# A refitted planner, a layernorm in steps and an in-place split in a two-layer hybrid backbone kernel

## The chip, the cores and the metric

The kernel is one program on one core of a Trainium2 chip. It has five engines with an instruction queue each: PE (TensorE, matrix products; its weight loads are shown as PEld), DVE (VectorE), ACT (ScalarE), POOL (GpSimd) and SP (SyncE, which issues most DMAs). The metric is the device time of one execution in microseconds (us), the median of several runs.

## The reference

Two layers act on 256 latent tokens and 256 context tokens of width 1024. Each layer modulates both streams, forms one wide input projection, runs four bidirectional mixers, merges their outputs by gates and adds a ConvFFN, each half closed by a residual layernorm:

```python
for i in range(DEPTH):                                   # DEPTH = 2
    zl = _split_cols(_modulate(x, sh1, sc1) @ w_in[i])
    zc = _split_cols(_modulate(h_ctx, csh1, csc1) @ w_in[i])
    ret_c, ret_l = _retention(zc, zl, n_rows)
    hg_c, hg_l = _hgrn2(zc, zl, ...)
    gd_c, gd_l = _gdn(zc, zl, ...)                       # gated delta rule: triangular solves
    lr_c, lr_l = _rglru(zc, zl, ...)
    y_l = _merge([ret_l, hg_l, gd_l, lr_l], zl['merge_gate'], w_branch[i], w_out[i])
    x = _layernorm(alpha * x + g1 * y_l, ln_mix_g[i], ln_mix_b[i])
    f_l = _conv_ffn(_modulate(x, sh2, sc2), w_up[i], ...)
    x = _layernorm(alpha * x + g2 * f_l, ln_ffn_g[i], ln_ffn_b[i])
    # the context stream likewise, in all layers but the last

def _merge(branches, gate_logits, w_branch, w_out):
    merged = sum(gates[:, :, j] * (branches[j] @ w_branch[j]) for j in range(4))
    return merged @ w_out
```

All of it is float32.

## The kernel before

**Products.** A float32 product is made of three products of a shorter type (float32r): both operands are split into a high part, rounded by ACT, and a low part, the difference. For the weights this goes tile by tile. SP loads a tile `wraw` (128 x 1024, 4 at a time), ACT rounds it to `wH`, and DVE or POOL subtracts: `wL = wraw - wH`. The thread `splitter` (line 332) does this some tiles ahead; 395 tiles need a split, and a split is 128 x 1024 elements except in the last products of an FFN (768) and the small `gd_ab` tiles (128). The engine is chosen by `tt` (line 671): DVE if the estimate of its end there, plus a bias, is below that on POOL. The names of the products on PE are `gft` and `gtf` (input projection, output projection and second FFN product), `up` (first FFN product) and `mg_b` (branch times `w_branch`).

**Order.** The program is one straight list, written by a planner at build time. Work is cut into threads (Python generators that yield the engine and the operands of the next step). `account` (line 150) keeps an estimated clock per engine, for every instruction as it is written; `pump` (line 244) picks the step that could start first by these clocks, and steps of matrix products where no thread's step can start before PE is free. So durations written into `account` decide where each instruction stands in each engine's queue, and through `tt`, on which engine it runs. On the chip each queue runs in that order, whatever the clocks were.

**Stages.** In time order: the start; layer 0's input products and mixers; its merge; `w_out` with the first residual layernorm; its FFN; the FFN's layernorm with the start of layer 1; the same stages of layer 1, the last of them a layernorm and the stores. In the mixers the gated delta rule inverts 32 x 32 triangular blocks by a chain of 60 POOL instructions each time (tiles `gd_x`, `gd_z`), four times in the program.

**Residual layernorm.** `gy = gtf * grow` and `r = r + gy` empty a bank of `w_out`'s (or the FFN's) products, `st` takes its statistics. When four are there, `ln_rs` computes the reciprocal deviation by some ten small DVE instructions (`rq`, `rq_v`, `rq_i`, `rq_n`), and `post_ln` (line 873) applies gain and bias to the two halves of `r`, four DVE instructions of 128 x 1024. In the old kernel `post_ln` is a plain function: these four are written at one go, and no other thread's step comes between them. Then `modulate` normalises again (`bst`, `xn`), transposes on PE (`xmt`) and splits (`xmH`, `xmL`).

**Merge.** For each of the four branches (order `lru`, `ret`, `gdn`, `hg`), `load` in `merge_jobs` (line 1007) fetches four blocks of it from DRAM into `br`, and splits each into `brH` (ACT) and `brL` (DVE or POOL). In the old kernel a block is loaded, then split, then the next comes; for the first two branches of layer 0 the DMAs stand in SP's queue, for the others in POOL's, between its splits. `prods` runs the products; DVE multiplies by the gates (`mg_th`) and adds to `merged`. Before it writes the next bank it finishes the bank before it, of the same branch.

Of the kernel before, what the change touches and what calls it, by code (L numbers as in the profile page):

```python
# [39 lines left out]
TRACE = 0  # L40
SUB_POOL = 1
POOL_BIAS = 0.3
# [5 lines left out]
SPLIT_BIAS = 0.3  # L48
ORDER = ("gdn0", "lru", "gdn1", "hg0", "hg1", "ret0", "ret1")
MERGE = ("lru", "ret", "gdn", "hg")  # L50
# by layer: the instances that follow one another in a pool
# [4 lines left out]
# the second layer's modulation blocks that fill the layernorms' waits  # L56
# [5 lines left out]
# from an engine's end to the start of the one that waits for it  # L62
# [9 lines left out]
class _Eng:  # L72
    """An engine of nc; every call also goes to the order's estimate of the engines' clocks."""
# [30 lines left out]
class _Pair:  # L104
    """the context's and the latents' jobs of one block"""
# [9 lines left out]
class Net:  # L115
    def __init__(self, nc, tc, I, out, n_tiles, dbg=None, stop=None):
# [9 lines left out]
        self.table, self.n_ran = "exp", 0  # L126
        self.jobs, self.fill, self.sel = [], [], []
# [5 lines left out]
    # ------------------------------------------- estimate of the engines' clocks  # L133
    def after(self, table, name, key):
        """when an engine sees that a tile is written (rdy) or read (rd)"""
        return max([t + LAT[p][key] for p, t in table.get(name, {}).items()] + [0.0])

    def names(self, x):
        """what the estimate knows an operand by: its tile, and the blocks of 256 for the activations"""
# [10 lines left out]
    def account(self, key, name, a, k):  # L150
# [12 lines left out]
        if not dma:  # L163
            # engines take turns at a PSUM tile
            for x in ins:
                if x.space == PSUM:
                    t = max([t] + [e for p, e in self.rd.get(x.tensor.name, {}).items() if p != key])
        by = key
        if key == "PE":
            if name == "transpose":  # L170
                d = 0.11
            elif ins[0].dtype == F32R:
                d = (n if n >= 256 else 4 * n) / 2400.0
            else:
                d = max(4 * n / 2400.0, 0.2)
                if out.ap[0][1] == 32:
                    d *= 0.28
        elif dma:
# [5 lines left out]
            d = out.ap[0][1] * n * 4 / 360e3  # L184
# [9 lines left out]
        elif key == "DVE":  # L194
# [5 lines left out]
            if name == "copy_predicated" and src_ps:  # L200
                e *= 0.85
            if name == "reciprocal":
                e *= 6
            if name == "tensor_reduce" or name.startswith("bn"):
# [4 lines left out]
            d = 0.07 + e + 0.06 * len(sc)  # L209
        else:  # L210
            d = 0.14 + n * 2.1e-3
        if not dma:
# [4 lines left out]
        for x in inn:  # L217
            q = self.rd.setdefault(x, {})
            q[by] = max(q.get(by, 0.0), t + d)

# [16 lines left out]
    # ------------------------------------------------------------- the order  # L237
# [33 lines left out]
    def finish(self, t, bank=False):  # L271
        """emit the rest of a thread, or its steps up to the last use of its bank"""
# [4 lines left out]
    def limit(self, key, n):  # L277
        """at most n threads of a kind are under way"""
# [5 lines left out]
    def when(self, t):  # L284
        """the engine of a thread's next step and the time when its operands are there (None: it waits for other steps)"""
# [8 lines left out]
    # -------------------------------------------------- matrix products' stream  # L294
# [20 lines left out]
    def feed(self):  # L315
        """keep loads three tiles ahead and splits two tiles ahead of the tile in use"""
# [15 lines left out]
    def splitter(self):  # L332
        """thread: the loaded tiles' two float32r parts, one tile ahead of the tile in use"""
# [15 lines left out]
    def gemm_start(self):  # L349
        """when the next step of the matrix products can start (None: it waits for a thread's step)"""  # L350
# [1872 lines left out]
```

## Time and profile before

| what | us |
|---|---|
| median of 3 runs | 2274.57 |
| lowest and highest run | 2270.27, 2276.27 |
| span of the profiled execution | 2267.0 |
| PE busy in it | 2085.0 |
| DVE busy | 1503.0 |
| ACT busy | 870.1 |
| POOL busy | 717.8 |

The span runs from the first to the last instruction, so the runs' times lie a few us above it; the profiled execution's own time is not given beyond its span. In all there are 35537 instructions. A busy share is a mean over stages: the rows below cut the span by stage, since the same engine may pace one stage and be idle in the next. "PEclk" or "clock" is the granted clock of PE as a share of 2.4 GHz; at its lower level, 1.2 GHz, it is 0.5.

### The profile page before, as it was taken

What the parts mean: (1) busy time and instruction counts of PE and PEld (TensorE: products, weight loads), DVE (VectorE), ACT (ScalarE), POOL (GpSimd) and SP (SyncE); (2) the same over time, 40 slices, a digit from 0 to 9 for tenths busy, and PEclk for the clock granted to TensorE, in tenths of its full rate; (3) what the DMA queues carried; (4) which work ended last, traced back from release to release, by engine and by line L of the source; (5) the groups of instructions that cost most, each with busy time, mean ns of one, the idle gap of its engine ahead of it and who ended that gap; (6) DMA issues with size and microseconds to landing.
All of it is one profiled execution on the core that took longest, in us unless ns stands there. A gap on an engine that the chain in (4) does not pass through costs nothing.

```text
span 2267.0 us, 35537 instructions
## 1 busy us (share of the span) xinstructions
PE 2085.0 (92%) x14052; PEld 1819.1 (80%) x14052; DVE 1503.0 (66%) x2380; ACT 870.1 (38%) x1277; POOL 717.8 (32%) x606
## 2 busy tenths in 40 slices
PE   6999899999999989879999986998998999888997
PEld 4767677877898968768898885887888889877997
DVE  6677346444383868976646688786375485878877
ACT  4555223222233233334423434664243323324553
POOL 1227422631130434420010032483247243513511
PEclk9999999999999999979999998999999999999999
DMA  7655325443314257554232344354234413566553
GB/s 296 202 171 161 126 64 161 120 148 103 120 64 136 83 174 248 160 176 128 91 98 93 98 154 159 111 161 139 83 120 129 135 33 98 177 234 209 180 187 118
DMA packets 133384, 320.14 MB, mean 141 GB/s; under 512 B 32961, under 2 KB 55265, under 8 KB 133217
## 3 DMA queue, kind: packets, MB, share of 16 engines
q1 hardware_dynamic: 119600, 289.76, 39.5%
q0 software_dynamic: 3712, 13.03, 1.8%
q10 hardware_dynamic: 9904, 15.08, 1.8%
q8 instruction: 111, 1.82, 0.3%
q14 instruction: 57, 0.46, 0.1%
HBM read 294.70 MB, written 23.10 MB: 140 GB/s over the span
## 4 chain that ended last, share of the span: by engine, by line
PE 64%; DVE 18%; POOL 5%; DMA 5%; issue 4%; ACT 3%; SPq 0%; ACTq 0%; DVEq 0%; POOLq 0%
PE gft L82 18%; PE gtf L82 15%; PE up L82 14%; PE mg_b L82 3%; DVE r L82 2%; POOL gd_x L82 2%; POOL gd_z L82 2%; DVE ffy L82 2%; DMA wraw<-in_wt 2%; PE hg_s L82 2%; DVE rq L82 2%; PE gd_U L82 2%; PE gd_o L82 2%; DMA br<-brd 1%; PE modp L82 1%
## 5 line engine op out<-in xcount | busy, mean ns | idle before, releaser
L82 POOL TENSOR_TENSOR wL<-wraw,wH 128x1024 fp32r<-128x1024 f32 (+2 forms) x143 | 335.7, 2351 | 890.3 <-ACT wH L82 756.5
L82 ACT ACTIVATE wH<-wraw 128x1024 fp32r<-128x1024 f32 (+2 forms) x395 | 408.0, 1036 | 216.2 <-PE gtf L82 130.5
L82 DVE TENSOR_TENSOR wL<-wraw,wH 128x1024 fp32r<-128x1024 f32 (+1 forms) x252 | 328.3, 1307 | 122.6 <-ACT wH L82 122.1
L82 PE MATMUL gft<-xmH,wH 128*128 128x512 f32 (+1 forms) x544 | 214.3, 398 | 3.8 <-ACT wH L82 3.8
L82 PE MATMUL gft<-xmL,wH 128*128 128x512 f32 (+1 forms) x544 | 205.5, 382 | 0.0
L82 PE MATMUL gft<-xms,wH 128*128 128x256 f32 x1344 | 188.3, 293 | 12.4 <-ACT lru_g L82 4.6
L82 PEld LDWEIGHTS gft<-xms,wH 128*128 128x128 f32 x1344 | 173.9, 198 | 18.1 <-ACT lru_g L82 4.8
L82 DVE SCALAR_TENSOR_TENSOR ffy<-up,parf,ffy 128x255 f32<-128x255 f32 (+1 forms) x188 | 110.9, 590 | 84.2 <-ACT ffy L82 79.5
L82 PE MATMUL up<-xmH,wH 128*128 128x512 f32 (+1 forms) x400 | 146.5, 373 | 13.6 <-DVE ffy L82 6.8
L82 PE MATMUL up<-xmL,wH 128*128 128x512 f32 (+1 forms) x400 | 146.1, 372 | 1.7 <-DVE xmL L82 1.7
L82 PEld LDWEIGHTS gft<-xmH,wH 128*128 128x128 f32 x544 | 103.7, 191 | 41.4 <-issue 16.7
L82 PE MATMUL gtf<-wH,hidH 128*128 128x256 f32 x528 | 132.0, 282 | 0.3 <-ACT wH L82 0.3
L82 PE MATMUL gtf<-wH,hidL 128*128 128x256 f32 x528 | 131.7, 282 | 0.0
L82 PE MATMUL gft<-xmH,wL 128*128 128x512 f32 (+1 forms) x544 | 131.3, 383 | 0.2 <-POOL wL L82 0.2
L82 PE MATMUL gtf<-wH,xmH 128*128 128x256 f32 x448 | 117.6, 294 | 9.6 <-DVE gy L82 9.0
L82 PEld LDWEIGHTS gft<-xmL,wH 128*128 128x128 f32 x544 | 103.8, 191 | 17.8 <-issue 0.7
L82 PEld LDWEIGHTS gft<-xmH,wL 128*128 128x128 f32 x544 | 98.2, 190 | 19.9 <-issue 1.3
L82 PE MATMUL gtf<-wH,xmL 128*128 128x256 f32 x448 | 113.6, 285 | 0.0
L82 ACT ACTIVATE ffy<-up,parf 128x256 f32<-128x256 f32 (+1 forms) x94 | 61.0, 648 | 120.2 <-PE up L82 120.0
L82 PE MATMUL mg_b<-brH,wH 128*128 128x256 f32 (+1 forms) x288 | 92.1, 338 | 13.4 <-ACT brH L82 9.1
L82 PEld LDWEIGHTS gtf<-wH,hidH 128*128 128x128 f32 x528 | 100.0, 189 | 0.6 <-ACT wH L82 0.5
L82 PEld LDWEIGHTS up<-xmH,wH 128*128 128x128 f32 x400 | 78.7, 197 | 26.7 <-issue 12.8
(335 smaller groups left out, 4677.9 us busy)
## 6 DMA issues: line engine op xcount, KB each, us to landing
wraw<-in_wt SPq DMA_DIRECT2D x467, 512.0 KB, 3.8
thd<-mg_t ACTq DMA_DIRECT2D x32, 256.0 KB, 2.2
mg_th<-thd SPq DMA_DIRECT2D x32, 256.0 KB, 4.1
wraw<-in_wt SPq DMA_DIRECT2D x20, 384.0 KB, 3.0
lnw<-in_rows POOLq DMA_DIRECT2D x8, 512.0 KB, 6.3
thd<-mg_t ACTq DMA_DIRECT2D x32, 128.0 KB, 2.6
xmm<-thd SPq DMA_DIRECT2D x16, 256.0 KB, 6.5
brd<-ro_b SPq DMA_DIRECT2D x28, 128.0 KB, 1.9
```

Of the source, the lines that this page charges most:

```text
L82: r = f(*a, **k)
```

## The change

1. `account` has other durations. A PE product takes 0.0135 us (float32r) or 0.01 us (float32) more, a change of PE's tiling mode 0.095 us, and `clocked` lets the estimated PE clock halve when it was idle. Two forms on DVE cost other amounts. `port` makes POOL instructions and DVE instructions with two SBUF operands (and single-operand `tensor_scalar` and copies) take turns in the estimate.
2. `POOL_BIAS` and `SPLIT_BIAS` go from 0.3 to -1.0: DVE is taken even if it would end up to 1 us later than POOL.
3. `post_ln` is a generator that yields before each half of `r`, so other steps can come between the halves; its callers use `yield from`.
4. A branch's block is loaded straight into the tile `brL`, all four DMAs first, and split in place; there is no `br` tile.
5. The bank before the next is finished across branches, too (`mlast`).

Docstrings and comments were also taken out, which the cut below leaves away.

```diff
-POOL_BIAS = 0.3
+POOL_BIAS = -1.0
-SPLIT_BIAS = 0.3
+SPLIT_BIAS = -1.0
...
         if key == "PE":
+            up = lambda z: 32 if z <= 32 else 64 if z <= 64 else 128
+            mode = up(ins[0].ap[0][1]), up(out.ap[0][1])
             if name == "transpose":
                 d = 0.11
             elif ins[0].dtype == F32R:
-                d = (n if n >= 256 else 4 * n) / 2400.0
+                mode = 128, 128
+                d = (n if n >= 256 else 4 * n) / 2400.0 + 0.0135
             else:
-                d = max(4 * n / 2400.0, 0.2)
+                d = max(4 * n / 2400.0, 0.2) + 0.01
                 if out.ap[0][1] == 32:
                     d *= 0.28
+            if mode != self.mode:
+                self.mode = mode
+                d += 0.095
+            d = self.clocked(t, d)
...
-            if name == "copy_predicated" and src_ps:
-                e *= 0.85
+            if name == "copy_predicated":
+                e = n * 1.13e-3
...
+            if name == "tensor_tensor_scan":
+                e = n * 2.1e-3
...
             d = 0.07 + e + 0.06 * len(sc)
+            if self.port_op(name, ins, sc):
+                t = self.port(key, t, d)
         else:
             d = 0.14 + n * 2.1e-3
+            t = self.port(key, t, d)
...
+    def clocked(self, t, d):
+        h, e = self.ham, t
...
+            f = 2.0 if h[2] else 1.0
...
+    def port(self, key, t, d):
+        q = self.turns
+        for k, s, e in q:
+            if k != key and s <= t < e:
+                t = e
+        q.append((key, t, t + d))
+        del q[:-6]
+        return t
...
         for j in range(2):
             x = r[:, j, :]
+            yield "DVE", [rs]
             V.scalar_tensor_tensor(x, in0=x, scalar=mv[:, j, 0:1], in1=self.lw[:, 0, :], op0=ALU.subtract, op1=ALU.mult)
...
-            st["L"] = self.tile(pool, [128, 4, n], F32R, "brL", "brL", nb)
+            st["L"] = self.tile(pool, [128, 4, n], F32, "brL", "brL", nb)
             for k in range(4):
-                b = self.ev([128, n], "br32") if early else self.tile(pool, [128, n], F32, "br32", "br32", 4)
-                (self.S if early else self.G).dma_start(b, self.brd[j][:, k, tsl])
-                yield "ACT", [b, st["H"]]
-                self.split(st["H"][:, k, :], st["L"][:, k, :], b)
+                (self.S if early else self.G).dma_start(st["L"][:, k, :], self.brd[j][:, k, tsl])
+            for k in range(4):
+                yield "ACT", [st["L"], st["H"]]
+                self.split(st["H"][:, k, :], st["L"][:, k, :].bitcast(F32R), st["L"][:, k, :])
...
                     if step == 1:
+                        self.finish(self.mlast)
                         if m == 0:
                             load_th(0)
-                        else:
-                            self.finish(st["rb", m - 1][0])
                         load_th(m + 1)
...
             self.evac(st["rb", m], pb, ev, "DVE")
+            self.mlast = st["rb", m][0]
```

The instructions are the same in number and kind; what moves is their order and, for DVE and POOL, their engine. Of the 395 `wL` splits, POOL has 143 before and 57 after. By the product that uses the tile, in program order, POOL's share is: start 8 and now 3; mixers of layer 0 20 and 12; merge 0 13 and 1; `w_out` of layer 0 9 and 5; first `up` tiles 7 and 5; the FFN's first half of `gtf` tiles 4 and 0, the last 10 and 5; first input products of layer 1 8 and 6; its mixers 30 and 15; merge 1 8 and 2; `w_out` 3 and 2; FFN 1 23 and 1.

POOL's queue in merge 0, before, around the loads of the last branch (`br` are its blocks, `brd_1` their place in DRAM; `brd_2` is the branch before it; `r`, `grow` and `lnw` are loads for the layernorm):

```order
L82 DMA br_7239<-brd_1_426 128x512
L82 DMA br_7254<-brd_1_426 128x512
L82 TENSOR_TENSOR wL<-wraw,wH 128x1024
L82 DMA br_7274<-brd_1_426 128x512
L82 TENSOR_TENSOR wL<-wraw,wH 128x1024
L82 TENSOR_TENSOR brL<-br_7274,brH 128x512
L82 DMA br_7325<-brd_1_426 128x512
L82 TENSOR_TENSOR wL<-wraw,wH 128x1024
L82 TENSOR_TENSOR brL<-br_7325,brH 128x512
L82 DMA r<-in_ctx 128x1024
L82 TENSOR_TENSOR wL<-wraw,wH 128x1024
L82 DMA r<-in_ctx 128x1024
```

Now, from the last mixer instruction on POOL to the first splits for `w_out`:

```order
L85 TENSOR_TENSOR hg_Q<-hg_Q,hg_G 128x8x64
L85 DMA brL<-brd_2_427 128x512 x4
L85 DMA brL<-brd_1_426 128x512 x4
L85 DMA r<-in_ctx 128x1024 x2
L85 DMA grow<-rowd_111 128x1024
L85 DMA r<-in_x 128x1024 x2
L85 DMA grow<-rowd_111 128x1024
L85 TENSOR_TENSOR wL<-wraw,wH 128x1024 x3
L85 DMA lnw<-in_rows 128x1024 x2
```

The loads now stand together, straight into `brL`, and the splits that stood between them and after them are gone up to `w_out`.

DVE's queue in the last branch of merge 0, before (one bank of products is `mg_th`, `merged`, `xmL`):

```order
L82 SCALAR_TENSOR_TENSOR mg_th<-mg_th,mg_b 128x512
L82 TENSOR_TENSOR merged<-merged,mg_th 128x2x256
L82 TENSOR_TENSOR xmL<-merged,xmH 128x2x256
L82 SCALAR_TENSOR_TENSOR mg_th<-mg_th,mg_b 128x512
L82 TENSOR_TENSOR merged<-merged,mg_th 128x2x256
L82 TENSOR_TENSOR wL<-wraw,wH 128x1024
L82 TENSOR_TENSOR xmL<-merged,xmH 128x2x256
L82 TENSOR_TENSOR wL<-wraw,wH 128x1024
L82 SCALAR_TENSOR_TENSOR mg_th<-mg_th,mg_b 128x512
```

And now, in the same branch:

```order
L85 SCALAR_TENSOR_TENSOR mg_th<-mg_th,mg_b 128x512
L85 TENSOR_TENSOR merged<-merged,mg_th 128x2x256
L85 TENSOR_TENSOR wL<-wraw,wH 128x1024
L85 TENSOR_TENSOR xmL<-merged,xmH 128x2x256
L85 SCALAR_TENSOR_TENSOR mg_th<-mg_th,mg_b 128x512
L85 TENSOR_TENSOR merged<-merged,mg_th 128x2x256
L85 TENSOR_TENSOR wL<-wraw,wH 128x1024
L85 TENSOR_TENSOR xmL<-merged,xmH 128x2x256
L85 SCALAR_TENSOR_TENSOR mg_th<-mg_th,mg_b 128x512
L85 TENSOR_TENSOR merged<-merged,mg_th 128x2x256
```

A weight split stands in each bank's work, between `merged` and `xmL`, where `xmL` before followed at once.

DVE's queue at the start of layer 1, in the context's layernorm of FFN 0; before (the four `r` are `post_ln`, `gd_yqk` and `gd_yv` the convolutions of the gated delta rule, which empty banks of PE):

```order
L82 SCALAR_TENSOR_TENSOR rq_n_12092<-rq_12089,rq_n_12087 128x2
L82 SCALAR_TENSOR_TENSOR r<-r,mv_12076,lnw 128x1024
L82 SCALAR_TENSOR_TENSOR r<-r,rq_n_12092,lnw 128x1024
L82 SCALAR_TENSOR_TENSOR r<-r,mv_12076,lnw 128x1024
L82 SCALAR_TENSOR_TENSOR r<-r,rq_n_12092,lnw 128x1024
L82 SCALAR_TENSOR_TENSOR gd_yqk<-gft,par_103,gd_yqk 128x254
L82 SCALAR_TENSOR_TENSOR gd_yqk<-gft,par_103,gd_yqk 128x255 x2
L82 SCALAR_TENSOR_TENSOR gd_yv<-gft,par_103,gd_yv 128x254
L82 SCALAR_TENSOR_TENSOR gd_yv<-gft,par_103,gd_yv 128x255 x2
L82 SCALAR_TENSOR_TENSOR gd_yv<-gft,par_103,gd_yv 128x254
L82 SCALAR_TENSOR_TENSOR gd_yv<-gft,par_103,gd_yv 128x255 x2
L82 BN_STATS bst<-r 128x6 x4
```

And now:

```order
L85 SCALAR_TENSOR_TENSOR rq_n_12076<-rq_12073,rq_n_12071 128x2
L85 TENSOR_TENSOR wL<-wraw,wH 128x1024
L85 SCALAR_TENSOR_TENSOR gd_yqk<-gft,par_103,gd_yqk 128x254
L85 SCALAR_TENSOR_TENSOR gd_yqk<-gft,par_103,gd_yqk 128x255 x2
L85 SCALAR_TENSOR_TENSOR r<-r,mv_12060,lnw 128x1024
L85 SCALAR_TENSOR_TENSOR r<-r,rq_n_12076,lnw 128x1024
L85 SCALAR_TENSOR_TENSOR gd_yv<-gft,par_103,gd_yv 128x254
L85 SCALAR_TENSOR_TENSOR gd_yv<-gft,par_103,gd_yv 128x255 x2
L85 SCALAR_TENSOR_TENSOR gd_yv<-gft,par_103,gd_yv 128x254
L85 SCALAR_TENSOR_TENSOR gd_yv<-gft,par_103,gd_yv 128x255 x2
L85 SCALAR_TENSOR_TENSOR r<-r,mv_12060,lnw 128x1024
L85 SCALAR_TENSOR_TENSOR r<-r,rq_n_12076,lnw 128x1024
```

The convolution `gd_yqk` moved ahead of the four `r`, the two pairs of `r` are apart, and a weight split came in ahead of them.

## Rows read from the trace of the kernel before

**Rows 1.** The page, parts 1 and 4: busy time by engine; chain shares.

```profile
PE 2085.0 (92%) x14052; PEld 1819.1 (80%) x14052; DVE 1503.0 (66%) x2380; ACT 870.1 (38%) x1277; POOL 717.8 (32%) x606
...
PE 64%; DVE 18%; POOL 5%; DMA 5%; issue 4%; ACT 3%; SPq 0%; ACTq 0%; DVEq 0%; POOLq 0%
PE gft L82 18%; PE gtf L82 15%; PE up L82 14%; PE mg_b L82 3%; DVE r L82 2%; POOL gd_x L82 2%; POOL gd_z L82 2%; DVE ffy L82 2%; DMA wraw<-in_wt 2%; PE hg_s L82 2%; DVE rq L82 2%; PE gd_U L82 2%; PE gd_o L82 2%; DMA br<-brd 1%; PE modp L82 1%
```

**Rows 2.** Windows, one a stage: length, busy by engine, granted clock, DMA.

```profile
core 0: us, PE busy (x) PEld busy (x) DVE busy (x) ACT busy (x) POOL busy (x), PEclk, DMA share, GB/s
...
57.00:826.00 769.00, 739.71 (x4452) 596.32 (x4450) 424.73 (x757) 265.68 (x395) 249.19 (x240) 0.98 0.40 128
826.00:907.00 81.00, 76.08 (x413) 66.03 (x414) 67.58 (x66) 26.51 (x33) 38.31 (x25) 0.92 0.70 240
907.00:1018.00 111.00, 83.18 (x638) 78.08 (x637) 96.23 (x152) 38.98 (x56) 38.30 (x23) 0.86 0.51 167
1018.00:1309.00 291.00, 290.67 (x1609) 254.64 (x1608) 179.64 (x220) 113.06 (x146) 12.34 (x8) 1.00 0.32 101
1309.00:1420.00 111.00, 86.23 (x701) 79.26 (x701) 97.56 (x161) 42.65 (x59) 35.24 (x16) 0.92 0.50 167
1420.00:1927.00 507.00, 471.57 (x3553) 434.39 (x3552) 327.49 (x534) 209.61 (x333) 225.77 (x220) 0.97 0.35 111
1927.00:2058.00 131.00, 107.72 (x822) 95.13 (x820) 105.24 (x153) 43.96 (x60) 44.23 (x32) 0.91 0.62 210
2058.00:2165.00 107.00, 102.58 (x830) 101.04 (x831) 87.48 (x105) 54.98 (x84) 53.75 (x26) 0.99 0.59 190
```

**Rows 3.** Windows, two stages, `wL` alone: length, PE, PEld, DVE, POOL busy (x).

```profile
826.00:907.00 81.00, 31.05 (x139) 23.64 (x140) 4.87 (x4) 30.19 (x13) 0.92 0.70 240
...
2058.00:2165.00 107.00, 42.59 (x280) 37.56 (x280) 20.42 (x17) 47.54 (x20) 0.99 0.59 190
```

**Rows 4.** Groups by form, DVE, then POOL: count, busy, mean ns, idle before.

```profile
L82 DVE TENSOR_TENSOR wL<-wraw,wH 128x1024 fp32r<-128x1024 f32 x247 | 323.6, 1314 | 121.5 <-ACT wH L82 121.1
...
L82 DVE SCALAR_TENSOR_TENSOR r<-r,gy 128x512 f32<-128x512 f32 x36 | 54.5, 1514 | 1.2
...
L82 DVE TENSOR_TENSOR merged<-merged,mg_th 128x512 f32<-128x512 f32 x24 | 39.9, 1663 | 0.8
...
L82 POOL TENSOR_TENSOR wL<-wraw,wH 128x1024 fp32r<-128x1024 f32 x124 | 305.5, 2467 | 553.3 <-ACT wH L82 511.8 <-DVE ffy L82 19.1 <-PE gtf L82 10.5
```

**Rows 5.** Timeline of DVE in merge 0: start, duration, instruction.

```profile
888.77 0.69 DVE L82 TENSOR_TENSOR merged<-merged,mg_th 128x512 f32<-128x512 f32 x1
...
890.16 0.69 DVE L82 TENSOR_TENSOR xmL<-merged,xmH 128x512 fp32r<-128x512 f32 x1 [0.69 <-ACT xmH L82]
...
891.48 2.60 DVE L82 TENSOR_TENSOR merged<-merged,mg_th 128x512 f32<-128x512 f32 x1
```

**Rows 6.** Timeline of POOL, the same stretch.

```profile
891.15 2.38 POOL L82 TENSOR_TENSOR wL<-wraw,wH 128x1024 fp32r<-128x1024 f32 x1 [7.66 <-ACT wH L82]
```

**Rows 7.** Waits of PE: who waited for whom, total us, times, longest.

```profile
PE gd_Tt L82 <- DVE gd_T L82: 10.2, 4, 8.3
...
PE mg_b L82 <- ACT brH L82: 9.1, 5, 3.6
PE gtf L82 <- DVE gy L82: 9.0, 1, 9.0
...
PE gd_ab L82 <- DVE gd_yqk L82: 5.8, 1, 5.8
...
PE mg_b L82 <- ACT wH L82: 4.2, 1, 4.2
```

**Rows 8.** Tile `br`: its loads from issue to landing, in us.

```profile
DMA to landing us min/median/max: 3.2/4.6/7.0
```

**Rows 9.** Timeline of POOL in a triangular chain of layer 0.

```profile
197.15 0.53 POOL L82 TENSOR_TENSOR gd_x<-gd_z 64x184 f32<-64x184 f32 x1
...
230.21 1.53 POOL L82 TENSOR_TENSOR gd_x<-gd_z 64x184 f32<-64x184 f32 x1
```

More of the change, by code (lines that the diff above doesn't have):

```diff
@@ L40 @@
 TRACE = 0
+DEBUG = 0
+DMA_RATE = 360e3
+WIN = 3.4133
 SUB_POOL = 1
-POOL_BIAS = 0.3
+POOL_BIAS = -1.0
 SUBST = 2.0
@@ L126, in __init__ @@
         self.table, self.n_ran = "exp", 0
+        self.mode, self.turns, self.ham = (128, 128), [], [0, 0.0, False]
         self.jobs, self.fill, self.sel = [], [], []
@@ L168, in account @@
         by = key
+        if DEBUG and key == "PE":
+            cand = [(c[key], "self")] + [(self.base.get(x, 0.0), "slot " + x) for x in on] + [(e + LAT[p][key], p + " rd " + x) for x in on for p, e in self.rd.get(x, {}).items()]
+            cand += [(e + LAT[p][key], p + " " + x) for x in inn for p, e in self.rdy.get(x, {}).items()]
+            self.dbg_t = (t, max(cand)[1].rsplit("_", 1)[0])
         if key == "PE":
+            up = lambda z: 32 if z <= 32 else 64 if z <= 64 else 128
+            mode = up(ins[0].ap[0][1]), up(out.ap[0][1])
             if name == "transpose":
@@ L183, in account @@
                 c[key] = self.hw
-            d = out.ap[0][1] * n * 4 / 360e3
+            d = out.ap[0][1] * n * 4 / DMA_RATE
             t = max(c[key] + 0.7, c["DMA"])
@@ L219, in account, with port_op @@
             q[by] = max(q.get(by, 0.0), t + d)
+    def clocked(self, t, d):
+        h, e = self.ham, t
+        while d > 1e-9:
+            w = int(e / WIN)
+            if w != h[0]:
+                a = h[1] / WIN if w == h[0] + 1 else 0.0
+                h[2] = a < (0.8 if h[2] and w == h[0] + 1 else 0.5) and e > 12.0
+                h[0], h[1] = w, 0.0
+            f = 2.0 if h[2] else 1.0
+            x = min((w + 1) * WIN - e, d * f)
+            h[1] += x
+            e += x + 1e-9
+            d -= x / f
+        return e - t
+    @staticmethod
+    def port_op(name, ins, sc):
+        big = [x for x in ins if x.space != PSUM and x not in sc]
+        return len(big) > 1 or (name in ("tensor_scalar", "tensor_copy") and len(big) == 1)
+    def port(self, key, t, d):
[6 more added lines that the diff above has]
+        return t
     def tile(self, pool, shape, dt, tag, name, bufs):
@@ L942, in mixers @@
         self.inst, self.first, self.mjobs, self.br_there = {}, [], {}, 0
-        self.merges, self.merged = False, None
+        self.merges, self.merged, self.mlast = False, None, None
         J = {}
@@ L1069, in prods @@
             for q in range(nd):
-                for _ in self.gemm_ft(pb[:, q, :], W, lambda k: [(st["H"][:, k, a:e], 0)], lambda k: [(st["L"][:, k, a:e], 0)], 4, 256, c0 + q * 128):
+                for _ in self.gemm_ft(pb[:, q, :], W, lambda k: [(st["H"][:, k, a:e], 0)], lambda k: [(st["L"][:, k, a:e].bitcast(F32R), 0)], 4, 256, c0 + q * 128):
                     yield
@@ L1149, in mid @@
             yield "DVE", [self.r[sg], self.lw]
-            self.post_ln(sg, None)
+            yield from self.post_ln(sg, None)
             yield "DVE", [self.r[sg]]
@@ L1168, in end @@
                 dst = (lambda t: self.xd2[t]) if sg == 1 else None
-            self.post_ln(sg, dst)
+            yield from self.post_ln(sg, dst)
             if not last:
```

## The prediction

> **What bounds the kernel now.** I read the page's busy times and chain first [rows 1]. PE is busy for 92% of the span, but in the chain that ended last it has 64%: the rest is time in which PE waited for somebody, and the largest share of it, 18%, is DVE's. POOL has 5%, of which the triangular chain's two tiles have 2% each. So a change of order can move only what PE waits, and the clock that falls after such waits. The windows by stage say where that is [rows 2]. FFN 0 (1018 to 1309) has PE busy for 290.67 of 291 us: nothing to gain there. The lost time is, stage by stage, length minus PE's busy time: mixers of layer 0 29.3 us, merge 0 4.9, `w_out` with the first layernorm 27.8, end of FFN 0 with the start of layer 1 24.8, mixers of layer 1 35.4, merge 1 to the second layernorm 23.3, first half of FFN 1 4.4. These make 149.9 us. The granted clock says the rest: it is 0.86 in the first layernorm's stage and 0.92 in two others, so part of the busy time there was run at 1.2 GHz. A share h of half clock gives a mean of 1 - h/2; at 0.86 that is h = 0.28, or 31 of 111 us, in which work was done that at 2.4 GHz needs half of it. A shorter wait gives back more than itself there.
>
> Who ends the waits is in the waits view [rows 7]: DVE tiles for the most part (`gd_T` 10.2 us, `gy` 9.0, `gd_yqk` 5.8), ACT's rounding of a branch (`brH`, 9.1 us in 5 waits) or of a weight (`wH`, once 4.2).
>
> What makes DVE late is in the groups [rows 4]. Of DVE's two-input instructions, `merged` takes a mean of 1.663 us; alone it takes 0.69, but 2.60 when a POOL weight split starts just ahead of it [rows 5]: that split ran from 891.15 to 893.53 [rows 6], and `merged`, begun at 891.48, ended at 894.08. It waited POOL out. `r<-r,gy` has the same pattern, a mean of 1.514 us.
>
> **The change, part by part.** 86 of 143 POOL splits go to DVE. What a POOL split costs DVE I work out in merge 0: 24 `merged` at 1.663 - 0.69 us above their time alone make 23.3 us, beside 13 POOL splits [rows 3, 4], so 1.8 us each. A split on DVE takes a mean of 1.31 us [rows 4]. A move saves DVE 0.5 us where both stand in its way, 43 us over 86 moves. It is not 43 us of time: it counts only in the 18%, and it is negative where POOL's split stretched nothing on DVE (saving 0, cost 1.31).
>
> The Trainium skill, "SBUF — State Buffer", section "Who interferes with whom", says the same as a rule: a DVE instruction with two SBUF inputs and a POOL one that reads SBUF exclude each other for the whole of whichever starts first. The trace agrees for DVE [rows 5, 6]. The rule speaks against the change too, since a split is such a DVE instruction and holds POOL up in turn; what that could do here is the second rival below.
>
> Now by stage, with the number of splits that POOL keeps.
>
> Merge 0 (13, now 1). DVE's work on a bank is three instructions of one size, `mg_th`, `merged` and `xmL`. With the 0.69 of the last two [rows 5] for all, it is 0.69 + 2.60 + 0.69 = 4.0 us beside a POOL split, and 3 x 0.69 + 1.31 = 3.4 with a DVE split. That split now stands between `merged` and `xmL`, where DVE otherwise waits 0.69 for ACT [rows 5]. The `wH` that PE waited 4.2 us for stands in ACT's queue behind `xmH`, which needs `merged`. Twelve moves give DVE 6 us. At most the stage's 4.9 us of waits and what its clock of 0.92 cost, 0.08 x 81 = 6.5 us, can go, 11.4 together. I take -4, between -10 and +3 (DVE then the slower of the two all through the last branch).
>
> Branch loads. Before, the loads went block by block with a split between, and the next branch's could start ahead of its turn, into `br`. Now all four go at once, but into `brL` itself, which the products of the branch before must have left where there is one such tile (layer 0, `lru` to `ret`). I put one landing, 4.6 us (3.2 to 7.0) [rows 8], plus a first split in place of waits of 9.1 us in all [rows 7]. In POOL's queue the eight loads of the last two branches no longer stand behind splits of 2.47 us [rows 4]. I take -2, between -4 and +5 (the old waits were partly other branches', and a new one of 7.0 comes on top).
>
> `w_out` and the first layernorm (16 with the first `up` tiles, now 10). In the latents' layernorm chain itself the order has 4 POOL splits and 1 DVE split before, 2 and 3 now: 4 x 1.8 + 1.3 = 8.5 us against 3.6 + 3.9 = 7.5. That is -1 on the chain and something off the half clock. I take -3, between -9 (a third of the 27.8) and +5 (three splits ahead of the chain with nothing saved).
>
> End of FFN 0 and start of layer 1 (18, now 11). The layernorm chain has 5 and 0 before, 2 and 3 now: 9.0 against 7.5 us. The wait of 5.8 us for `gd_yqk` goes in part: its convolution now stands ahead of the four `r`, but behind one weight split, 1.31 us. What is late next is the context's own layernorm, through which the instructions on DVE stay the same, so I count 2 of these 5.8. Sum with the clock of 0.92: -5, between -12 and +5.
>
> Merge 1 to the second layernorm (11, now 4). As in layer 0, but the layernorm's own chain had no POOL split: -3, between -9 and +4.
>
> FFN 1 (23, now 1). In its first half 20 POOL splits cost DVE 20 x 1.8 = 36 us of stall at most, and PE waits 4.4 us in all [rows 2]; DVE would have 87.48 + 26.2 - 36 = 78 us of work in 107, and up to 114 if the stalls stay. I take -3, between -4.4 and +6.
>
> Mixers (layer 0: 20, now 12; layer 1: 30, now 15). 23 moves save POOL 57 us and DVE some 11. Waits are 64.7 us; most are ends of long chains through PE, ACT, DVE and POOL, in which one split is one link. The planner's other costs (PE's longer products, its clock) also set here which product fills a wait, which no row prices. I take a sixth of the waits, -10, between -32 (half) and +20 (a third more).
>
> Start, FFN 0 and the last layernorm: 0. `post_ln` in steps has its effect inside the two layernorm stages; `mlast` and the tiling modes I cost at nothing, since no wait in the rows is theirs.
>
> Sum: -4 - 2 - 3 - 5 - 3 - 3 - 10 = -30 us on the profiled span of 2267.0. The median of the runs, 2274.57, is 7.6 above it; I put the sum on the median: 2245 us.
>
> **Rivals.** First, more goes: if the planner now sees both the exclusion and PE's real pace, half of the 149.9 us can go, as 75 us: 2200. For it: 8.3 of the wait for `gd_T` and 9.0 for `gy` are one wait each [rows 7]. Against: each layernorm's chain is DVE work that no order shortens.
>
> Second, the gain is eaten in the mixers. A link of the triangular chain, `gd_x` 64 x 184, takes 0.53 us alone and 1.53 beside DVE's work [rows 9]. If each of the 23 moved splits holds up one link for 1.0 us and these links are on the chain that ends last (4% of it is theirs [rows 1]), the mixers lose 23 us instead of gaining 10: -20 + 23 = +3, 2278, which cannot be told from no change. Against it: the chain in layer 0 also loses a POOL split of its own. The rule of the skill named above would give this; the trace bears it out for single links.
>
> Third, slower: DVE's queue becomes what PE waits for. 86 splits at 1.31 us are 113 us more in a queue in which they stand by order ahead of other work, in merge 0 between `merged` and `xmL`, in layer 1 ahead of `gd_yqk`. With DVE's 18% of the chain that is +20 us; with a lost early load (+5) 2300. It decides where the split stands ahead of chain work and the stall it removes is under 1.3 us, that is, where POOL's split had run beside an idle DVE or work that it does not stretch. For it: DVE is busy for 96.23 of 111 us in the first layernorm's stage. Against it: 1.8 is above 1.31 in merge 0.
>
> That the order does not change is excluded by the counts.
>
> **How the numbers follow.** Forecast (2222 to 2267) 0.56; more goes 0.14; no change 0.13; slower 0.17. The runs of the kernel before span 6 us, so 0.3% or 6.8 us is about what can be told. Faster takes the first two and a little less for the edge: 0.70; same 0.13; slower 0.17. The bounds of the terms all at their good ends would give 2274.6 - 80, at their bad ends + 48; not all fall together. The range that leaves a tenth out on either side goes from 2194 to 2290; the likeliest case's own is 2222 to 2267.
>
> **What would show it.** Right: `merged` and `r<-r,gy` near 0.9 us in the mean; PE's granted clock above 0.90 in the first layernorm's stage; no wait of 4 us for `wH` in merge 0; the wait for `gd_yqk` shorter. Wrong: `gd_x` and `gd_z` longer in the mean, or a larger share for them in the chain (second rival); DVE tiles as releasers of more of PE's wait than before, or PE waiting for a `wL` that DVE made (third); a wait of over 5 us for `brH` at the second branch. Wrong altogether would be a gain from the mixers alone, or a gain in a stage whose splits have not moved.

## The result, and the profile after

The changed kernel takes a median of 2244.11 us (2242.12 to 2249.27, 4 runs), against 2272.42 (2264.49 to 2276.27) for the kernel before in the same comparison: a ratio of 0.9887, 95% interval 0.9863 to 0.9912. The forecast was 2245. As the sections below show, the sum came out right and its mechanism, that a split on POOL costs DVE more than one of its own, was confirmed by fixing the order and moving the splits alone; but of the seven terms only that of merge 1 came out at its size, and the sum was near by offset.

The page of the changed kernel, its first lines and the line of busy times, answers to [rows 1]:

```profile
span 2240.4 us, 35464 instructions
## 1 busy us (share of the span) xinstructions
PE 2076.6 (93%) x14052; PEld 1812.5 (81%) x14052; DVE 1497.5 (67%) x2524; ACT 871.7 (39%) x1277; POOL 438.9 (20%) x462
```

POOL lost 279 us of work; DVE took over 86 splits and is busy for 5.5 us less than before. The counts of the five engines are those of before, DVE and POOL taken together; the 73 instructions fewer are none of theirs. PE's work is the same and takes 8.4 us less, at a mean granted clock of 0.970 instead of 0.964; and what it waits (span minus busy) fell from 182.0 to 163.8 us.

The groups by form, as in [rows 4]: the splits on DVE, `r<-r,gy` and `merged`, and the splits left on POOL (count, busy us, mean ns).

```profile
L85 DVE TENSOR_TENSOR wL<-wraw,wH 128x1024 fp32r<-128x1024 f32 x319 | 405.8, 1276 | 149.9 <-ACT wH L85 149.7
...
L85 DVE SCALAR_TENSOR_TENSOR r<-r,gy 128x512 f32<-128x512 f32 x36 | 31.4, 872 | 1.2
...
L85 DVE TENSOR_TENSOR merged<-merged,mg_th 128x512 f32<-128x512 f32 x24 | 22.0, 918 | 0.8
...
L85 POOL TENSOR_TENSOR wL<-wraw,wH 128x1024 fp32r<-128x1024 f32 x52 | 127.3, 2449 | 566.0 <-ACT wH L85 512.1 <-DVE rq_i L85 36.7 <-DVE gd_B L85 17.0
```

`r<-r,gy` fell from a mean of 1514 ns to 872, `merged` from 1663 to 918, as the prediction asked ("near 0.9 us").

The windows of the changed kernel, with the columns of [rows 2]: merge 0, `w_out` with layer 0's first layernorm up to the first `up` product, the end of FFN 0, the start of layer 1, merge 1 without its `w_out`, and FFN 1.

```profile
777.00:887.30 110.30, 105.47 (x599) 89.80 (x598) 89.42 (x142) 34.75 (x46) 15.47 (x19) 0.98 0.65 217
887.30:953.10 65.80, 52.21 (x403) 50.77 (x401) 59.32 (x86) 25.29 (x30) 16.93 (x9) 0.94 0.49 163
1286.20:1359.60 73.40, 68.14 (x544) 67.11 (x544) 63.04 (x91) 30.23 (x36) 15.45 (x7) 0.95 0.48 148
1359.60:1423.20 63.60, 45.60 (x363) 37.56 (x361) 52.85 (x120) 26.23 (x48) 9.59 (x6) 0.89 0.51 174
...
1911.70:1979.60 67.90, 59.27 (x473) 57.56 (x473) 50.45 (x80) 24.50 (x34) 17.13 (x18) 0.97 0.67 219
2033.20:2226.80 193.60, 191.04 (x1585) 190.63 (x1584) 158.89 (x248) 105.81 (x155) 3.94 (x4) 0.99 0.58 180
```

Cut at the same products of PE in both kernels (first and last `mg_b`, first and last `up`, last product of the FFN, and the last transpose of layer 1's `gd_ab`), the two profiled executions compare as follows, in us. These cuts differ a little from those of [rows 2], and the sum is that of the spans, 2240.4 - 2267.0.

| stage | before | after | difference | forecast |
|---|---|---|---|---|
| start and mixers 0 | 776.2 | 777.0 | +0.8 | with mixers 1: -10 |
| mixers 1 | 493.9 | 488.5 | -5.4 | |
| merge 0 | 126.5 | 110.2 | -16.3 | -4 - 2 |
| `w_out`, layernorm, FFN 0 up to its last group of `gtf` | 399.2 | 399.0 | -0.2 | -3 |
| end of FFN 0 | 77.1 | 73.4 | -3.7 | -5 |
| start of layer 1 | 56.2 | 63.6 | +7.4 | (in the -5) |
| merge 1 to the second layernorm | 124.2 | 121.5 | -2.7 | -3 |
| FFN 1 | 200.2 | 193.6 | -6.6 | -3 |
| tail | 13.5 | 13.6 | +0.1 | 0 |

### The profile page after: what moved, and what is told of

Read it like the earlier page. It is cut to its first block, busy times and chain, and to the rows that moved or that the text cites. A ratio compares the mean times of both kernels' runs of the same rounds, so it can differ in the third digit from the quotient of the medians.

```text
span 2240.4 us, 35464 instructions
## 1 busy us (share of the span) xinstructions
PE 2076.6 (93%) x14052; PEld 1812.5 (81%) x14052; DVE 1497.5 (67%) x2524; ACT 871.7 (39%) x1277; POOL 438.9 (20%) x462
## 5 line engine op out<-in xcount | busy, mean ns | idle before, releaser
L85 DVE TENSOR_TENSOR wL<-wraw,wH 128x1024 fp32r<-128x1024 f32 x338 | 422.4, 1253 | 150.3 <-ACT wH L85 150.0
L85 POOL TENSOR_TENSOR wL<-wraw,wH 128x1024 fp32r<-128x1024 f32 (+2 forms) x57 | 135.0, 2369 | 901.5 <-ACT wH L85 841.2
L85 PE MATMUL gtf<-wH,hidL 128*128 128x256 f32 x528 | 132.0, 282 | 0.0
L85 PEld LDWEIGHTS gtf<-wH,hidL 128*128 128x128 f32 x528 | 100.1, 190 | 0.1
L85 PE MATMUL gft<-xms,wL 128*128 128x256 f32 x672 | 96.5, 290 | 3.3 <-DVE wL L85 3.3
```

Of the source, the lines that this page charges most:

```text
L85: r = f(*a, **k)
```

## The experiments

Each was run in five rounds beside the kernel before; a ratio is to it, with its 95% interval. First the stages of each run's profile, in us, at the cuts above. "LN 0" is `w_out` of layer 0 to the first `up`, "start 1" is the end of FFN 0 with the start of layer 1, "LN 1" is merge 1 to the second layernorm, "on POOL" the weight splits there. The stages of FFN 0 between "LN 0" and "start 1", and the tail, are left out. The stages are of one execution of each kernel, which took from 5 us less (e2) to 10 us more (e6) than the median, so a few us in a stage alone tell little.

| kernel | on POOL | ratio | mixers 0 | merge 0 | LN 0 | start 1 | mixers 1 | LN 1 | FFN 1 |
|---|---|---|---|---|---|---|---|---|---|
| before | 143 | 1 | 776.2 | 126.5 | 64.3 | 133.3 | 493.9 | 124.2 | 200.2 |
| changed | 57 | 0.9887 | 777.0 | 110.2 | 65.9 | 137.0 | 488.5 | 121.5 | 193.6 |
| e1 biases only | 65 | 1.0019 | 772.2 | 120.5 | 74.3 | 136.2 | 481.6 | 128.9 | 207.5 |
| e2 no refit | 65 | 0.9989 | 764.4 | 115.3 | 72.7 | 129.7 | 494.9 | 128.3 | 208.9 |
| e3 no biases | 142 | 1.0070 | 785.7 | 126.9 | 70.3 | 132.5 | 504.4 | 124.7 | 202.9 |
| e4 no in-place loads | 51 | 1.0047 | 788.6 | 116.1 | 66.0 | 130.6 | 519.0 | 119.4 | 193.8 |
| e5 engine only | 0 | 0.9824 | 777.9 | 125.2 | 59.3 | 130.7 | 480.4 | 122.1 | 190.9 |
| e6 no PE refit | 56 | 1.0091 | 794.8 | 115.5 | 72.8 | 130.1 | 503.3 | 127.3 | 211.8 |
| e7 planner, none on POOL | 0 | 0.9795 | 789.1 | 114.8 | 60.1 | 131.7 | 475.9 | 122.8 | 190.8 |
| e8 no half clock | 53 | 0.9929 | 777.5 | 113.4 | 65.9 | 132.0 | 510.9 | 123.4 | 191.6 |
| e9 splits put back | 143 | 1.0030 | 775.8 | 116.6 | 67.3 | 138.8 | 503.7 | 128.4 | 203.0 |
| e10 rest on DVE | 0 | 0.9695 | 769.9 | 110.6 | 59.7 | 132.3 | 466.6 | 124.2 | 190.7 |
| e11 steps only | 143 | 1.0002 | 777.0 | 127.7 | 64.7 | 131.5 | 500.9 | 124.8 | 200.2 |
| e12 nothing on POOL | 0 | 0.9738 | 775.8 | 104.1 | 61.9 | 132.8 | 477.0 | 119.8 | 191.2 |

**One part alone, or all but one.** The first four runs asked which part carries the gain. What e1 and e4 compute is off (relative error 0.022 and 1.34, for a reason that isn't known), so their times are those of programs that may lack a wait; nothing below rests on them alone.

```diff
# e1, on the kernel before
-POOL_BIAS = 0.3
+POOL_BIAS = -1.0
-SPLIT_BIAS = 0.3
+SPLIT_BIAS = -1.0
```

> The kernel before with the two biases at -1.0 and nothing else of the change; POOL keeps 65 of 143 weight splits. Theory A (POOL's splits stood in DVE's way, 1.8 us each against 1.3 on DVE): most of the gain is here, 2244 to 2256, and merge 0 (126.6 us before, 110.3 in the changed kernel) falls to 112 to 117. Theory B (the loads of the branches, all four at once and in place, made merge 0 shorter): merge 0 keeps its two waits for brH of 2.9 and 3.6 us and the low clock behind them and stays at 117 or more; in all 2258 to 2268. Theory C (the refitted estimates set a better order): within 6 us of before.

Measured: 2273.01 us, ratio 1.0019 (1.0010 to 1.0029). Theory A in its simple form (each split moved off POOL gains) fails: 78 splits moved and nothing was gained. Merge 0 gained 6 us; `LN 0` lost 10 and FFN 1 lost 7.

```diff
# e2, on the changed kernel: the old durations back, no clocked(), no port() (cut)
-                d = (n if n >= 256 else 4 * n) / 2400.0 + 0.0135
+                d = (n if n >= 256 else 4 * n) / 2400.0
...
-                d += 0.095
-            d = self.clocked(t, d)
...
-            t = self.port(key, t, d)
```

> The changed kernel with the old estimates of time (no longer products, no half clock, no turns between DVE and POOL, old copy_predicated and scan); biases, steps, in-place loads as changed; POOL keeps 65 splits. Theory A: 2242 to 2252, merge 0 at 108 to 114. Theory C: the gain is gone for the most part, 2262 or more, with waits of PE back at other places.

Measured: 2267.35 us, ratio 0.9989 (0.9975 to 1.0004). Theory C's number. The same two stages are long as in e1: 72.7 and 208.9. It computes the reference's result and has 78 splits fewer on POOL too, with no gain, so what is said of e1 stands on e2 as well.

```diff
# e3, on the changed kernel
-POOL_BIAS = -1.0
+POOL_BIAS = 0.3
-SPLIT_BIAS = -1.0
+SPLIT_BIAS = 0.3
```

> The changed kernel with the two biases back at 0.3; POOL has 142 splits again. Theory A: 2262 to 2276, mean of r<-r,gy and merged above 1.3 us again, merge 0 above 118. Theory B: merge 0 at 110 to 114 though the splits are back. Theory C: 2245 to 2255.

Measured: 2284.25 us, ratio 1.0070 (1.0053 to 1.0088), slower than any theory had it. Merge 0 is back at 126.9, so theory B's loads in place don't shorten it beside POOL's splits. Neither the biases (e1, and e2 with the steps and the loads) nor the refit without them (e3) has any gain of its own: together they give 1.1%.

```diff
# e4, on the changed kernel (cut; the bank before the next is finished within a branch alone, as before)
-                (self.S if early else self.G).dma_start(st["L"][:, k, :], self.brd[j][:, k, tsl])
+                b = self.ev([128, n], "br32") if early else self.tile(pool, [128, n], F32, "br32", "br32", 4)
+                (self.S if early else self.G).dma_start(b, self.brd[j][:, k, tsl])
+                self.split(st["H"][:, k, :], st["L"][:, k, :], b)
```

> The changed kernel with the branches' blocks loaded one by one into a tile of their own and split from there, and banks finished within a branch alone, as before; POOL has 51 splits. Theory A: merge 0 within 5 us of the changed kernel's 110.3, in all 2240 to 2252. Theory B: waits for brH of 6 us or more in all are back in merge 0, which is at 118 or more, in all 2252 to 2262.

Measured: 2280.20 us, ratio 1.0047 (1.0030 to 1.0065). Merge 0 is at 116.1, 6 us over the changed kernel, between what A and B asked. The edit takes back two parts, the loads in place and the finish across branches, and lets the planner answer; which of the three the 6 us are isn't shown. But the loss is in the mixers: 788.6 and 519.0, 42 us more than in the changed kernel, in a part of the program that this edit changes only by what the planner does next. That the planner's order of the mixers is this sensitive none of the theories had.

**The engine alone, with the order held.** To part the order from the engine I let the planner go as before and only issue the splits elsewhere, at the same place of the program (`tt`, which picks the engine, is at line 618 of the kernel before and at line 671 of the changed one):

```diff
# e9 and e10 on the changed kernel (cut); e5, on the kernel before, likewise for the splits put on POOL
         def call(*a, **k):
-            r = f(*a, **k)
+            on = getattr(self._net, "on", None)     # set around a weight split: the engine it goes to
+            g = getattr(dict(DVE=self._net.V, POOL=self._net.G)[on]._eng, name) if on else f
+            r = g(*a, **k)
             self._net.account(self._key, name, a, k)
```

> The kernel before, its order and its planner's clocks untouched, but each of the 143 weight splits that it put on POOL is issued on DVE at the same place of the program. Theory A (a POOL split costs DVE more than a DVE split): merge 0 (126.5 us before) at 113 to 118, FFN 1 (200.2) at 193 to 196, in all 8 to 22 us below the kernel before. Theory D (what counts is where the splits stand in DVE's queue, which only the planner that knows of it sets right): merge 0 and FFN 1 gain, but the two stages with w_out and a layernorm and the start of layer 1 lose 4 us or more each, in all within 7 us of the kernel before or above it.

The traces show the order held: without the weight splits, the sequences on PE, ACT, DVE and POOL are those of the kernel before in e5 and those of the changed kernel in e9 and e10, but for the place of one or two instructions.

Measured: 2232.03 us, ratio 0.9824 (0.9809 to 0.9840), 38.9 us below the kernel before, well over theory A's 8 to 22, and 12 below the changed one, without any of its order. Theory A's direction is shown for FFN 1 (190.9) and for the layernorm stages, which by theory D should have become longer: `LN 0` is 5 us shorter, start 1 2.6. Merge 0 is not as A had it: 125.2. In that order its two waits for `brH` and the one for `wH` stay. PE's waits for the merge, in e5:

```profile
PE mg_b L89 <- ACT brH L89: 8.1, 4, 3.3
...
PE mg_b L89 <- ACT wH L89: 3.3, 1, 3.3
```

Against 9.1 and 4.2 before [rows 7]. With no POOL split in the way of `merged` these remain, so they are the order's: ACT's queue has three `wH` behind a row of `xmH`. The timeline of ACT in e5 shows it (start, duration, instruction):

```profile
889.80 0.63 ACT L89 ACTIVATE xmH<-merged 128x512 fp32r<-128x512 f32 x1 [2.08 <-DVE merged L89]
890.33 2.94 ACT L89 ACTIVATE wH<-wraw 128x1024 fp32r<-128x1024 f32 x3
```

In the changed kernel each `wH` follows one `xmH`:

```profile
878.55 0.63 ACT L85 ACTIVATE xmH<-merged 128x512 fp32r<-128x512 f32 x1 [1.48 <-DVE merged L85]
879.09 1.04 ACT L85 ACTIVATE wH<-wraw 128x1024 fp32r<-128x1024 f32 x1
```

**Which part of the refit, and how far to go.** The next three look at the refit and at the end of the road.

```diff
# e6, on the changed kernel
-                d = (n if n >= 256 else 4 * n) / 2400.0 + 0.0135
+                d = (n if n >= 256 else 4 * n) / 2400.0
-                d = max(4 * n / 2400.0, 0.2) + 0.01
+                d = max(4 * n / 2400.0, 0.2)
-                d += 0.095
```

> The changed kernel with the old estimates of PE's products and no price for a change of tiling mode; half clock, turns and DVE's two durations stay. In FFN 1 it leaves 9 splits on POOL, as the kernel without the whole refit, where the changed kernel leaves 1. Theory E (the refit works by PE's longer products: PE looks slower, so DVE looks less late and takes all splits of FFN 1): FFN 1 at 204 to 210 us, with waits for ffy of 2 to 3 us, and in all 2254 to 2268. Theory F (turns and half clock do it): FFN 1 at 193 to 196, in all 2240 to 2250.

Measured: 2290.23 us, ratio 1.0091 (1.0072 to 1.0110), worse than theory E had it, and its stage, FFN 1, is long as E said and a little more (211.8 us; `LN 0` 72.8, as in e1 and e2). With the old estimate PE looks faster, DVE looks late, and some splits in FFN 1 go to POOL again. Few are worse than many: with 22 or 23 on POOL (before, e3, e9, e11) the stage took 200 to 203 us, with 1 or none 191 to 194, and with 8 (e1, e2, e6; the expectation counted 9) 207.5 to 211.8. In e2 DVE is busy for 167 of its 208.9 us, against 161.5 of 200.2 before, PE's waits for `ffy` are 8.2 us against 2.2, and the granted clock is 0.96 against 0.99. What one of these 8 does, in e2: POOL's split, the DVE instructions beside it, and PE's wait.

```profile
2067.28 3.40 POOL L85 TENSOR_TENSOR wL<-wraw,wH 128x1024 fp32r<-128x1024 f32 x1 [5.32 <-ACT wH L85]
```

```profile
2067.21 1.21 DVE L85 TENSOR_TENSOR wL<-wraw,wH 128x1024 fp32r<-128x1024 f32 x1
2068.34 2.62 DVE L85 SCALAR_TENSOR_TENSOR ffy<-ffth,ffy 128x256 f32<-128x256 f32 x1
...
2075.36 0.41 DVE L85 SCALAR_TENSOR_TENSOR ffy<-ffth,ffy 128x256 f32<-128x256 f32 x1
```

```profile
2073.51 2.75 PE L85 MATMUL up<-xms,wH 128*128 128x256 f32 x12 [2.74 <-DVE ffy L85]
```

POOL's split began beside a DVE split and took 3.40 us, the `ffy` of 0.41 us then 2.62, until POOL was done at 2070.68, and PE waits 2.74 us for a later one.

```diff
# e7, on the changed kernel
-SPLIT_BIAS = -1.0
+SPLIT_BIAS = -99.0
# e8, on the changed kernel
-            d = self.clocked(t, d)
```

> The changed kernel with no weight split on POOL at all (57 in the changed kernel). Theory A: the layernorm stages gain 1 to 3 us each, FFN 1 stays at 193 to 195, in all 2234 to 2244. Rival (DVE's queue becomes what PE waits for): the stages with w_out and a layernorm are 4 us or more longer each, PE's waits for DVE's wL grow, in all 2250 or more.

Measured: 2223.60 us, ratio 0.9795 (0.9775 to 0.9815). Better than theory A's range; the rival (DVE's queue too long) is out for the kernel as a whole.

> The changed kernel with the planner's PE clock never halved; 53 splits on POOL, FFN 1 with one, as changed. Theory E: FFN 1 at 193 to 195 and merge 0 within 3 us of the changed kernel's 110.2; in all 2238 to 2252, any difference lying in the mixers, whose order moves most. Theory F: 2256 or more.

Measured: 2256.10 us, ratio 0.9929 (0.9912 to 0.9946), just inside theory F's range (2256 or more) and above theory E's. But its stages are nearer to E: FFN 1 takes 191.6, merge 0 113.4, 3.2 over the changed kernel; mixers 1 takes 510.9, 22 us more. Again the difference is in the mixers' order, so the total doesn't decide between the two.

**The converse, and the rest.**

> The changed kernel, its order on every queue as the planner wrote it, but the weight splits go to the engine that the kernel before gave to the split of the same number: 143 on POOL instead of 57. The opposite of the run with the old order and all splits on DVE, which took 38.9 us off, 0.27 us a split. Theory A (the engine of the split is what counts, in either order): 86 x 0.27 = 23 us more than the changed kernel, 2260 to 2274, with FFN 1 (193.6) above 198 and r<-r,gy above 1.3 us. Theory G (the new order is worth something by itself): 2246 to 2256.

Measured: 2277.60 us, ratio 1.0030 (1.0016 to 1.0044): 33 us over the changed kernel, above theory A's range. FFN 1 is at 203.0, `r<-r,gy` at a mean of 1461 ns. So with the old engines the new order is worth nothing as a whole. Merge 0 is the exception, at 116.6: 10 of its 16 us stay with the splits back on POOL, so they are the order's and the loads', which the runs don't part.

> The changed kernel with its order kept, and the 57 splits that it leaves on POOL issued on DVE at the same place. Theory A: 57 x 0.27 = 15 us less than the changed kernel, 2222 to 2234, as the kernel whose planner knew of it (2223.6). Theory G (the planner left on POOL only what disturbs nothing): 2239 to 2247.

Measured: 2200.47 us, ratio 0.9695 (0.9676 to 0.9715), well below theory A's range, and the fastest of all. The last 57 splits were worth 43.6 us, 0.77 each, not 0.27. 29 of it is in the mixers (1265.5 to 1236.5 us for both layers), 6.2 in `LN 0` (by the profiled executions, 43.6 us apart too). What one split did there shows in the changed kernel, in a readout of the retention branch. POOL, then DVE (start, duration, instruction):

```profile
1715.28 0.62 POOL L85 TENSOR_TENSOR gd_z<-gd_z,gd_x 64x210 f32<-64x210 f32 x1
1715.86 2.40 POOL L85 TENSOR_TENSOR wL<-wraw,wH 128x1024 fp32r<-128x1024 f32 x1
```

```profile
1714.59 0.17 DVE L85 TENSOR_SCALAR rq_i<-rq_v 128x2 int32<-128x2 int32 x1
...
1715.26 0.16 DVE L85 TENSOR_TENSOR rq<-rq_i 128x2 f32<-128x2 f32 x1
1715.45 2.83 DVE L85 SCALAR_TENSOR_TENSOR rq<-rq,rq_v 128x2 f32<-128x2 f32 x1
```

An instruction on 2 elements a partition, 0.16 us in most of its 74 executions, took 2.83. It began beside an instruction of the triangular chain, the split came behind that, and it ended when the split was done at 1718.26; PE waited 4.4 us for the result (`ro_t<-ret_ob`). Such waits make 13.4 us in the changed kernel and 2.2 in e10, its last row here:

```profile
PE ro_t L85 <- DVE ret_ob L85: 13.4, 5, 4.4
```

```profile
PE ro_t L88 <- DVE ret_ob L88: 2.2, 2, 1.4
```

```diff
# e11, on the kernel before: post_ln a generator, its callers with yield from
+            yield "DVE", [rs]
# e12, on the changed kernel
-POOL_BIAS = -1.0
+POOL_BIAS = -99.0
-SPLIT_BIAS = -1.0
+SPLIT_BIAS = -99.0
```

> The kernel before with post_ln in steps and nothing else of the change; the splits stay at 143 on POOL. All theories: within 5 us of the kernel before, the end of FFN 0 with the start of layer 1 (133.3 us there) 1 to 4 us shorter, since the wait for gd_yqk goes and the context's layernorm stays as long. More than 8 us less would mean that the steps were a main part of the gain.

Measured: 2269.72 us, ratio 1.0002 (0.9988 to 1.0015). As expected: the start of layer 1 1.8 us shorter, the rest the planner's.

> The changed kernel with both biases so low that POOL keeps its triangular chains and DMAs alone; the hg_Q, hg_k, gd and hidL products that the planner could place go to DVE as well. Theory A carried on: 2212 to 2224, the mixers no longer than with the splits alone on DVE (789.1 and 475.9). The rival that DVE's queue becomes what PE waits for: the mixers 10 us or more longer together, PE's waits for hg_Q and hg_k grow, 2230 or more.

Measured: 2207.86 us, ratio 0.9738 (0.9713 to 0.9763), below theory A's range. The mixers together (1252.8) are 12 us shorter than in e7, so the further work on DVE doesn't lengthen them. It stays above e10, whose mixers take 1236.5.

## Why the prediction came out right, and where it did not

The main step holds: a POOL split costs DVE more than a split of its own. Its size was off. In e5 DVE is busy for 1477.1 us, of which `wL` takes 490.8; before it was 1503.0 and 328.3. The rest of DVE's work fell from 1174.7 to 986.3, 188.4 us for 143 splits or 1.32 each, where I had taken 1.8 from merge 0. A DVE split added (490.8 - 328.3) / 143 = 1.14 us, where I had 1.31. (Both are net of what the old DVE splits got shorter: the mean of a 128 x 1024 split on DVE is 1278 ns in e5, 1314 before.) The saving of 0.5 us of DVE time a move was 0.18.

"It is not 43 us of time: it counts only in the 18%" was wrong the other way. 143 moves save 26 us of DVE's busy time and 38.9 us of the kernel. A stall falls on whatever DVE does next, as on the `rq` above, and where that is a link of a chain PE waits for it. PE's clock gains as well: its mean is 0.964 before and 0.969 in e5, 0.964 in e9 and 0.977 in e10. The mean over DVE hides that.

PE's waits by who ended them say the same, and one thing more. In the kernel before, DVE's tiles end 92 us of them, in e5 61.5, of which 26 are for a `wL` that DVE now makes. A second cause, that POOL makes a `wL` in 2.4 us where DVE takes 1.3, is small beside that: PE waited 4.9 us for POOL's. In the changed kernel DVE's tiles still end 92 us, in a sum of waits that is 18 us shorter by ACT's and POOL's tiles. In its order with the old engines (e9) they ended 109: the order had added 17 us for DVE, and the 86 moves took them away. And 10.7 us of the 92 are for DVE's own `wL`, of which there were none before, a sign that the prediction had set for its third rival:

```profile
PE gtf L85 <- DVE wL L85: 6.0, 5, 2.2
...
PE gft L85 <- DVE wL L85: 4.1, 2, 3.3
```

Branch loads (-2) and merge 0 (-4): mis-sized, -16.3 together. The bound of "11.4 together" came from a window that begins at 826, 50 us into the merge. Over the whole merge, before, PE waits 14.2 us at a clock of 0.93, where the prediction counted 4.9 at 0.92 and left the rest in the mixers' term:

```profile
776.20:902.80 126.60, 112.35 (x614) 94.91 (x613) 96.33 (x128) 38.05 (x50) 55.02 (x39) 0.93 0.57 193
```

In the changed kernel it waits 4.8 us at 0.98. I put the 4.2 us for `wH` down to POOL by way of `merged`; e5 shows that it was the order of ACT's queue. And the loads in place, of which I feared a new wait of 7 us, left one of 1.4, where five before made 9.1 [rows 7]:

```profile
PE mg_b L85 <- ACT brH L85: 1.4, 1, 1.4
```

10 us are the order's and the loads', 6 the engine's (e9 against the changed kernel; in the old order the engine alone gave 1.3, e5).

End of FFN 0 and start of layer 1 (-5): the sign was wrong, +3.7. The step "its convolution now stands ahead of the four `r`" came true, and the wait of 5.8 us for `gd_yqk` is gone. It became another: PE arrives earlier at the modulation product `modr`, whose operand ACT makes behind the context's softplus chain. In the changed kernel, PE:

```profile
1387.58 1.01 PE L85 MATMUL modr<-modrow,sel 128*2 128x512 f32 x1 [9.03 <-ACT modrow L85]
```

and ACT, which stood for 4.79 us ahead of `sp_e` until DVE had done the layernorm ahead of `sp_ax`:

```profile
1383.57 0.22 ACT L85 ACTIVATE sp_e<-sp_ax 128x16 f32<-128x16 f32 x1 [4.79 <-DVE sp_ax L85]
1383.80 1.28 ACT L85 ACT_TABLE_LOAD   x1
...
1386.95 0.58 ACT L85 ACTIVATE modrow<-modp 128x512 f32<-128x512 f32 x1
```

"What is late next is the context's own layernorm" was right; that it had become longer, by the split and the convolutions between its steps, I had not counted. Before, the same wait was 3.2 us.

Mixers (-10, "a sixth of the waits", a share and no mechanism): -4.6, and of unknown cause: over the runs these two stages take anywhere from 1236 to 1308 us, 1288 with nothing changed but the half clock in the planner's estimate (e8). With the splits alone moved they give -11.8 (e5) and -29.0 (e10).

FFN 1 (-3, at best -4.4 for its first half): -6.6, and -9.3 in e5. PE's waits of before, 4.4 us in the window of the first half, weren't all: over the stage they fell from 7.0 to 2.6 us, and the same products took 193.22 us before and 191.04 now (e5: 190.84, at a clock of 1.00).

First layernorm (-3): -0.2. The prediction asked for a granted clock above 0.90 there as a sign; over the same 111 us of work it is 0.85, against 0.86 in [rows 2], in the changed kernel:

```profile
892.00:1003.00 111.00, 86.90 (x637) 79.32 (x638) 96.88 (x163) 41.29 (x59) 24.47 (x16) 0.85 0.52 174
```

DVE is as busy as before (96.88 and 96.23 us) though POOL does a third less: what the stalls gave back the splits took. e10's `LN 0` of 59.7 us shows what the splits still on POOL cost there.

The rivals. Second (POOL's triangular chain held up by moved splits): out. The chain's instructions, over the whole of each kernel (length, POOL busy, count), before and in e5 with 143 splits more on DVE:

```profile
0.00:2267.00 2267.00, 163.25 (x240) 0.96 0.44 141
```

```profile
0.00:2233.70 2233.70, 164.78 (x240) 0.97 0.44 143
```

They take 1.5 us more in all, not 23. But the test is a narrow one: within the four chains only three more DVE splits begin in e5 than before (31 against 28), while POOL's own five splits there are gone, and from first to last instruction the chains take 183.3 us instead of 196.5. What the prediction held against this rival, that the chain "also loses a POOL split of its own", is what e5 shows. Third (DVE's queue becomes the bound): false as put, since 143 more splits on DVE gain. Yet something of it is in e1, e2 and e6, where DVE has most splits, a few stay on POOL, and FFN 1 takes 208 to 212 us. First rival (more goes): it did not in this kernel, but e10's 2200.47 is what it forecast, by emptying POOL, not by the planner's better sight.

So that the number was right to 1 us is luck. It started from 2274.57, where this comparison's kernel before has 2272.42, so the change was -28.3 and not -30. Against the terms, merge 0 and FFN 1 gave 13.9 us more, and the first layernorm, the end of FFN 0 with the start of layer 1, merge 1 and the mixers 17.2 less. The engine's part was larger than the terms had it, and the planner's part about zero: by corners, with 143 splits on POOL the new order gives 1.0030 instead of 1, with none it gives 0.9695 instead of 0.9824. That last step, 1.3%, may be the order's real worth or the luck of one order among many; e7, whose planner knew that all splits go to DVE, has 0.9795. The runs don't part these.

## What to carry to other kernels

A helper engine that shares a path with the main one has a price that doesn't show as its own time: count what it stretches, and ask where in a chain that falls. Try none of it before balancing it: here the balance by end times, however refitted, lost to giving the helper nothing. And to learn what an order is worth, hold it fixed and change one thing under it; each run in which the planner was free to answer also changed stages that had nothing to do with the edit.

## What the runs showed of the hardware

In three cases a DVE instruction beside a POOL split waited until the split was done, whatever its own size: 128x2 elements took 2.83 us instead of 0.16, 128x256 2.62 instead of 0.41, 128x512 2.60 instead of 0.69 [rows 5]. In the first it had begun beside an earlier POOL instruction, and the split behind that still came before it. The other way round, a POOL split took 3.40 us beside a DVE split (e2) where another took 2.40, and a link of POOL's chain 1.53 instead of 0.53 [rows 9]. The Trainium skill, "SBUF — State Buffer", section "Who interferes with whom", has the two sides exclude each other alike, and these single instructions agree with it. The sums don't weigh the two directions: 188 us of DVE's time came back with the splits and the chains' instructions took 1.5 us more (163.25 to 164.78), but hardly any of the added DVE splits stood beside a chain.
